# Turning the memory attention's weights by VectorE and DRAM instead of by TensorE

## The chip, the cores and the metric

The kernel runs on one core of a Trainium2 chip. Its engines are TensorE (PE; its weight loads are listed apart as PEld), VectorE (DVE), ScalarE (ACT), GpSimd (POOL) and SyncE (SP). They run independently, each through its own list of instructions in order, and wait for one another by semaphores. The metric is the device time of one execution in microseconds (us); less is better.

## What is computed

Two layers of a decoder trunk on 256 tokens of width 1024, all in 32-bit floats. Each layer is a SwiGLU half step, three token mixers in parallel, and another half step, with layer norms between. The three mixers (gated DeltaNet, sliding-window attention, attention to a memory of 256 rows) read one projection of the same stream, and their results are merged by gates:

```python
def memory_cross_attention(q, mem_n, w_mem_kv):
    ...
    s = jnp.einsum('bshd,bmhd->bhsm', q, k).astype(jnp.float32) * (XA_DH ** -0.5)
    p = jax.nn.softmax(s, axis=-1)
    o = jnp.einsum('bhsm,bmhd->bshd', p.astype(v.dtype), v)

def gated_delta_rule(q, k, v, g, beta):
    ...
    t_mat = a + jnp.eye(C, dtype=f32)
    sol = lax.linalg.triangular_solve(t_mat, rhs, left_side=True, lower=True, unit_diagonal=True)
    ...

merged = jnp.sum(gates * jnp.einsum('bsnc,ncd->bsnd', branches, w_branch), axis=2)
h = layer_norm(DEEPNORM_ALPHA * h + merged @ w_out, ln_g[1], ln_b[1])
```

Four heads of 128 attend to the memory. The change touches how `p` is turned for the second einsum, and the order of the work for the triangular solve.

## The kernel before

**Products.** Every product with a weight matrix is made of three matmuls: operands are split into a high part (rounded, `whi`, `hi`) and a low part (the rest, `wlo`, `lo`), and high x high, high x low and low x high are added up. Weights come from one long stream in DRAM in units of 128 x 1024 (`unit`). SyncE fetches a unit into one of four `raw` buffers, ScalarE rounds it (line 125), VectorE takes the difference (also line 125). There are five buffers for each half. The accumulators are four PSUM banks (`acc`); small products use `sm` and `at`, two banks each.

**Order.** In the mixers TensorE's instructions stand in program order (`keep_in_program_order`). The order is written out by `weave(work, steps)`: `work` is a run of large products in steps (one unit of weights each), and behind step n the functions in `steps[n]` are put, so that small work lies between large products. On the other engines a scheduler puts the instructions in order when the program is built, by its own estimate of the time; on the chip each engine then keeps that order. `tc.issue_after(i)` holds what is recorded under it behind the instruction `i`.

**Memory attention.** `x_scores(tb)` computes scores and softmax of token block tb (128 tokens) and leaves the weights in a tile `pp`, tokens on the partitions. `x_turn(tb)` turns them so that memory rows lie on the partitions: for each half `kb` of the memory four transposes of 128 x 128 on TensorE (line 137, into `at`), and one copy out of PSUM into a tile `pt` (line 749, by ScalarE for kb = 0, by VectorE for kb = 1). `x_values(tb)` multiplies with the memory's values and splits the result into high and low halves, `oX` (tiles `u6` and `u7`; line 125: ScalarE writes the high half, VectorE the low one).

**Delta inverses.** The triangular solve is done by building the inverse of each 128-block's matrix. `products` leaves the matrices in `AK` (tiles `u12`, `u13`). `inverses` starts with the 16 x 16 blocks on the diagonal: VectorE masks and sums them into `cp` (lines 826 and 827), GpSimd sends `cp` to DRAM (`dr`, line 829) and reads it back twice as a broadcast to all partitions (into `TM`, tiles `w2` and `w3`, line 833). GpSimd then eliminates in 15 steps of two operations (lines 845 and 846) and writes the first blocks of the inverse to `Y32` in tile `w0` (line 847). Eight mask products into `L32` (line 836) are GpSimd's too; the first matmuls of `doubling` read them. `begin_inverse` lets VectorE turn these blocks (line 940), behind the second `w_scores`. The doubling steps then run on TensorE.

**The place of the change.** `gates(0)` is eight steps of gate products; `branch(0, oX)` behind it projects the memory attention's result: four units of weights, then for block 0 and for block 1 two accumulators of 12 matmuls each, whose results VectorE takes out (line 1036). The matmuls of block 1 read the halves of `oX` that `x_values(1)` wrote. Transfers of GpSimd stand in its list like its other instructions: it waits there until their data are ready, issues them, and goes on. `leave_v` and `back_v` (lines 605 and 610) already turn other data the way that the change uses: VectorE's stream transpose turns each 32 x 32 block, four transfers bring the blocks to DRAM in the new order, and one reads them back.

Of the kernel before, what the change touches and what calls it, by code (L numbers as in the profile page):

```python
# [17 lines left out]
P = 128  # L18
# [20 lines left out]
def tile_trunk(ctx, tc, x, xT, mem, memT_, wst, lnp, memln, cvw, rows, cst, out):  # L39
# [484 lines left out]
    def mixers(l, hT, mkT, mv_, post):  # L524
# [197 lines left out]

        def x_scores(tb):
# [19 lines left out]
        def x_turn(tb):  # L743
            pT = prs[2 + tb] = T(p2, [P, 2, 4, P], "pt")
            for kb in range(2):
                ps = at().rearrange("p (h k) -> p h k", h=4)
                for h in range(4):
                    transpose(ps[:, h, :], prs[tb][:, h, kb * P:(kb + 1) * P], ident)
                (nc.vector.tensor_copy if kb else nc.scalar.copy)(pT[:, kb], ps)

        def x_values(tb):
            if not oX:
                oX.extend(T(pu, [P, 4, S], tag, F32R) for tag in ("u6", "u7"))
            ts = slice(tb * P, (tb + 1) * P)
            ps = at().rearrange("p (h k) -> p h k", h=4)
            for h in range(4):
                for kb in range(2):
                    matmul(ps[:, h, :], mv_[:, kb, h * P:(h + 1) * P], prs[2 + tb][:, kb, h, :], start=kb == 0, stop=kb == 1)
            split(oX[0][:, :, ts], oX[1][:, :, ts], ps)
# [61 lines left out]
        def inverses():  # L821

            cp = T(p2, [P, 2, 4, 16], "t2", bufs=4)
# [5 lines left out]
            nc.gpsimd.dma_start(dr, cp.rearrange("p c h i -> p (c h i)"))  # L829
            blocks = dr.rearrange("(d j) n -> d (j n)", j=16)  # L830
            for t in range(2):
                src = blocks[:, t * 1024:(t + 1) * 1024].unsqueeze(1).to_broadcast([8, 16, 1024])
                nc.gpsimd.dma_start(TM[t].rearrange("p a h c -> p (a h c)"), src)
            for c in range(2):
                for q in qd:
                    nc.gpsimd.tensor_tensor(L32[q, c], AK[c][q, :, 0, q], cs[q, C_LV:C_LV + 32].unsqueeze(1).to_broadcast([32, 4, 32]), op=ALU.mult)

            y16 = T(p2, [P, 8, 16], "t2", bufs=4)
            pr16 = T(p2, [P, 8, 15], "t2", bufs=4)
            i16 = cs[:, C_I16:C_I16 + 16].unsqueeze(1).to_broadcast([P, 8, 16])  # L840
            nc.gpsimd.tensor_copy(y16, i16)
# [22 lines left out]
        for kv in range(2):  # L864
# [5 lines left out]
            3: [lambda: spread(1)],  # L870
# [152 lines left out]
        def branch(n, o):  # L1023
# [19 lines left out]
            3: [lambda: x_turn(0)],  # L1043
            4: [lambda: x_values(0)],
            5: [lambda: x_turn(1)],
            6: [lambda: x_values(1)],
            7: [lambda: w_scores(0, 0)],
            8: [lambda: w_scores(0, 1)]})
# [193 lines left out]
```

## Time and profile before

| what | value |
|---|---|
| median of three runs | 1273.09 us (1271.39 to 1273.2) |
| the profiled execution's own time | 1271.84 us |
| its span, first to last instruction | 1270.1 us |
| granted TensorE clock, mean | 0.999 |
| TensorE busy | 1258.1 us |
| GpSimd busy | 221.0 us |

How to read the lines of the profile: the page gives, for each engine, busy time, share of the span and number of instructions; then the chain of work that ended last, followed back from the last instruction. A row of the timeline has start and length in us, engine, line, operation, result tile<-operand tiles, shapes and a count; in brackets stands the idle time of the engine just before it and what ended it. A row of a group ends with busy time and mean ns of one, then the idle time before. For transfers it gives the size of one and the median us from issue to landing. A row of the view by stretches has a stretch of time, the busy us of PE, PEld, DVE, ACT and POOL, the granted clock, and the share and speed of DMA.

### The profile page before, as it was taken

The page shows a single profiled execution, that of the slowest core. Times are in us where ns is not written, and L with a number is a line of the kernel's source. Part 1 is how long each engine was busy: PE and PEld are TensorE (multiplying, and loading weights), DVE is VectorE, ACT ScalarE, POOL GpSimd, SP SyncE. Part 2 cuts the span into 40 slices and gives each one's busy share as a digit, 9 for nine tenths or more (in the row PEclk, how much of TensorE's full clock was granted, in tenths as well). Part 3 has the DMA queues.
Part 4 walks back from the last instruction along what each step waited for, and adds up shares of the span by engine and source line. Part 5 has one row for each costly group of instructions (what it writes and reads, how often), then busy time and mean ns, then how long its engine had stood idle before and what let it go on. Part 6 is the DMA issues. An engine that isn't in the chain of part 4 may idle for free.

```text
span 1270.1 us, 18774 instructions
## 1 busy us (share of the span) xinstructions
PE 1258.1 (99%) x6916; PEld 1070.9 (84%) x6916; DVE 871.3 (69%) x1284; ACT 661.5 (52%) x982; POOL 221.0 (17%) x395
## 2 busy tenths in 40 slices
PE   9999999999999999999999999999999999999997
PEld 7888889999878888888888888899987788888886
DVE  6678576886667776665666665759776588766565
ACT  6456444655664544454454554455646654454441
POOL 1233000002331102221012220000023401122100
PEclk9999999999999999999999999999999999999999
DMA  8988765655554648787668887566554456578771
GB/s 293 322 265 286 249 210 160 205 179 137 164 151 150 240 139 258 243 242 220 215 208 246 256 255 216 178 185 212 162 158 133 134 189 226 174 248 243 240 231 74
DMA packets 78795, 263.56 MB, mean 208 GB/s; under 512 B 12528, under 2 KB 13968, under 8 KB 78704
## 3 DMA queue, kind: packets, MB, share of 16 engines
q1 hardware_dynamic: 66320, 232.40, 56.5%
q0 software_dynamic: 12240, 29.84, 8.7%
q8 instruction: 54, 0.88, 0.3%
q14 instruction: 37, 0.30, 0.1%
q10 hardware_dynamic: 144, 0.13, 0.0%
HBM read 247.48 MB, written 14.85 MB: 207 GB/s over the span
## 4 chain that ended last, share of the span: by engine, by line
PE 94%; DVE 3%; DMA 2%; ACT 1%; issue 1%; SPq 0%; DVEq 0%; ACTq 0%
PE acc L134 83%; PE at L134 3%; PE sm L134 3%; DMA raw<-in_wst_dram 2%; PE sm L137 1%; DVE wlo L125 1%; PE acc L335 1%; PE acc L332 1%; PE at L137 1%; PE acc L333 1%; ACT whi L125 1%; DVE h L291 0%; DVE h L296 0%; DVE h L418 0%; DVE bnst L277 0%
## 5 line engine op out<-in xcount | busy, mean ns | idle before, releaser
L125 DVE TENSOR_TENSOR wlo<-raw,whi 128x1024 fp32r<-128x1024 f32 (+2 forms) x405 | 487.1, 1210 | 277.0 <-ACT whi L125 275.0
L125 ACT CAST whi<-raw 128x1024 fp32r<-128x1024 f32 (+2 forms) x405 | 413.7, 1029 | 403.5 <-PE acc L134 314.8
L134 PE MATMUL acc<-whi,hT 128*128 128x512 f32 (+1 forms) x1824 | 563.1, 386 | 0.0
L134 PEld LDWEIGHTS acc<-whi,hT 128*128 128x128 f32 x1824 | 340.5, 188 | 68.9 <-issue 1.6
L134 PE MATMUL acc<-wlo,hT 128*128 128x512 f32 (+1 forms) x912 | 350.5, 384 | 0.1
L134 PE MATMUL acc<-whi,u 128*128 128x512 f32 x812 | 259.6, 392 | 0.0
L134 PEld LDWEIGHTS acc<-wlo,hT 128*128 128x128 f32 x912 | 171.6, 188 | 33.4 <-DVE wlo L125 0.9
L134 PEld LDWEIGHTS acc<-whi,u 128*128 128x128 f32 x812 | 152.3, 188 | 32.0 <-DVE u L125 0.5
L134 PE MATMUL acc<-wlo,u 128*128 128x512 f32 x406 | 158.2, 390 | 0.0
L362 POOL DMA_DIRECT2D tr<-t x176 | 96.0, 552 | 306.4 <-DVE t L356 299.4
L134 PE MATMUL acc<-hT,whi 128*128 128x256 f32 x672 | 121.8, 284 | 0.0
L134 PEld LDWEIGHTS acc<-hT,whi 128*128 128x128 f32 x672 | 104.7, 192 | 0.0
L134 PE MATMUL acc<-hT,wlo 128*128 128x256 f32 x336 | 95.1, 283 | 0.0
L134 PEld LDWEIGHTS acc<-wlo,u 128*128 128x128 f32 x406 | 76.3, 188 | 15.5
L134 PEld LDWEIGHTS acc<-hT,wlo 128*128 128x128 f32 x336 | 64.4, 192 | 0.0
L363 POOL DMA_DIRECT2D pt<-tr x44 | 25.0, 568 | 197.3 <-DMA tr<-t 151.6
L353 ACT ACTIVATE t<-acc 128x256 f32<-128x256 f32 x88 | 33.3, 379 | 37.1 <-PE acc L134 36.9
L134 PE MATMUL acc<-u,u 128*128 128x512 f32 x186 | 46.4, 394 | 0.0
L354 DVE TENSOR_TENSOR t<-t,acc 128x256 f32<-128x256 f32 x88 | 36.6, 417 | 8.1 <-ACT t L353 3.9
L134 PEld LDWEIGHTS acc<-u,u 128*128 128x128 f32 x186 | 34.6, 188 | 7.5
L553 DVE SCALAR_TENSOR_TENSOR t<-acc,cw,t 128x255 f32<-128x255 f32 (+2 forms) x72 | 34.5, 479 | 1.1
L125 DVE TENSOR_TENSOR u<-pt,u 128x512 fp32r<-128x512 f32 x44 | 28.9, 657 | 8.1 <-ACT u L125 8.1
(245 smaller groups left out, 1165.0 us busy)
## 6 DMA issues: line engine op xcount, KB each, us to landing
raw<-in_wst_dram SPq DMA_DIRECT2D x409, 512.0 KB, 4.4
tr<-t POOLq DMA_DIRECT2D x176, 64.0 KB, 3.9
pt<-tr POOLq DMA_DIRECT2D x44, 256.0 KB, 5.1
raw<-in_wst_dram SPq DMA_DIRECT2D x16, 324.0 KB, 3.0
gB<-in_lnp_dram SPq DMA_DIRECT2D x6, 512.0 KB, 6.7
bB<-in_lnp_dram SPq DMA_DIRECT2D x6, 512.0 KB, 7.0
w<-dr POOLq DMA_DIRECT2D x4, 512.0 KB, 12.6
t<-in_xT_dram SPq DMA_DIRECT2D x4, 256.0 KB, 5.4
```

What stands on the lines that cost most here:

```text
L125: return nc.scalar.copy(hi, src).ins, nc.vector.tensor_tensor(lo, src, hi.bitcast(F32), op=ALU.subtract).ins
L134: return pe(nc.tensor.matmul(*a, **k))
L137: return pe(nc.tensor.transpose(*a))
L332: nc.tensor.matmul(ps, hT[0][:, k, ts], hi[:, c], start=k == 0, stop=False)
L333: nc.tensor.matmul(ps, hT[0][:, k, ts], lo[:, c], start=False, stop=False)
L335: nc.tensor.matmul(ps, hT[1][:, k, ts], hi[:, c], start=False, stop=k == KD - 1)
L353: act = nc.scalar.activation(t[:, :, tb, :], g, AF.Silu).ins
L354: ins = nc.vector.tensor_tensor(t[:, :, tb, :], t[:, :, tb, :], u, op=ALU.mult).ins
L362: nc.gpsimd.dma_start(d[:, :, q].rearrange("b c x -> c b x"), z[32 * q:32 * q + 32].rearrange("c (b x) -> c b x", b=4))
L363: back = nc.gpsimd.dma_start(y, d.rearrange("b c q x -> (b c) (q x)")).ins
L553: nc.vector.scalar_tensor_tensor(yc[:, j, d:], b[:, j, :S - d], w[:, t:t + 1], yc[:, j, d:], op0=ALU.mult, op1=ALU.add)
```

## The change

The transposes of `x_turn` leave TensorE. VectorE turns the 32 x 32 blocks of each half of the weights, GpSimd sends them to DRAM by four transfers and reads them back by one (`square`). `x_turn(0)` now stands behind the third step of the run before `gates(0)`, ahead of `products(0, 0)`. `x_turn(1)` is no step of its own any more: `inverses` calls it and lays its transfers between its own, and `issue_after` ties GpSimd's list to that order, with the mask products behind all of them. `cp`, `y16` and `pr16` get tiles of their own. `x_values(0)` moves from step 4 to 5 of `gates(0)`, `w_scores(0, .)` from 7 and 8 to 6 and 7, and `x_values(1)` from 6 to 8, the last step ahead of `branch(0)`.

```diff
+        def square(src, dst, tag, after=None, bufs=2):
+
+            z = T(p2, [P, 512], "t2", bufs=4)
+            nc.vector.transpose(z, src)
+            d = T(pd, [4, 32, 4, P], tag, bufs=bufs)
+            for a in range(4):
+                nc.gpsimd.dma_start(d[:, :, a].rearrange("m x c -> x m c"), z[32 * a:32 * a + 32].rearrange("x (m c) -> x m c", m=4))
+            return lambda: nc.gpsimd.dma_start(dst, d.rearrange("m x a c -> (m x) (a c)"))
...
         def x_turn(tb):
-            pT = prs[2 + tb] = T(p2, [P, 2, 4, P], "pt")
-            for kb in range(2):
-                ps = at().rearrange("p (h k) -> p h k", h=4)
-                for h in range(4):
-                    transpose(ps[:, h, :], prs[tb][:, h, kb * P:(kb + 1) * P], ident)
-                (nc.vector.tensor_copy if kb else nc.scalar.copy)(pT[:, kb], ps)
+            pT = prs[2 + tb] = T(p2, [P, 2, 4, 4, 32], "pt")
+            backs = [lambda kb=kb: square(prs[tb][:, :, kb * P:(kb + 1) * P].rearrange("p h (m x) -> p m h x", m=4), pT[:, kb].rearrange("p a h x -> p (a h x)"), "tx", 4) for kb in range(2)]
+            if tb:
+                return backs
+            for f in [b() for b in backs]:
+                f()
...
-                    matmul(ps[:, h, :], mv_[:, kb, h * P:(h + 1) * P], prs[2 + tb][:, kb, h, :], start=kb == 0, stop=kb == 1)
+                    matmul(ps[:, h, :], mv_[:, kb, h * P:(h + 1) * P], prs[2 + tb][:, kb, :, h, :], start=kb == 0, stop=kb == 1)
...
-            nc.gpsimd.dma_start(dr, cp.rearrange("p c h i -> p (c h i)"))
+            sent = nc.gpsimd.dma_start(dr, cp.rearrange("p c h i -> p (c h i)")).ins
+
+            def then(f):
+                with tc.issue_after(sent):
+                    return f()
+
+            turns = x_turn(1)
+            backs = [then(turns[0])]
             blocks = dr.rearrange("(d j) n -> d (j n)", j=16)
             for t in range(2):
                 src = blocks[:, t * 1024:(t + 1) * 1024].unsqueeze(1).to_broadcast([8, 16, 1024])
-                nc.gpsimd.dma_start(TM[t].rearrange("p a h c -> p (a h c)"), src)
+                sent = then(lambda: nc.gpsimd.dma_start(TM[t].rearrange("p a h c -> p (a h c)"), src)).ins
+            backs.append(then(turns[1]))
+            for f in backs:
+                sent = then(f).ins
             for c in range(2):
                 for q in qd:
-                    nc.gpsimd.tensor_tensor(L32[q, c], AK[c][q, :, 0, q], cs[q, C_LV:C_LV + 32].unsqueeze(1).to_broadcast([32, 4, 32]), op=ALU.mult)
+                    ins = then(lambda: nc.gpsimd.tensor_tensor(L32[q, c], AK[c][q, :, 0, q], cs[q, C_LV:C_LV + 32].unsqueeze(1).to_broadcast([32, 4, 32]), op=ALU.mult)).ins
+            sent = ins
...
-            nc.gpsimd.tensor_copy(y16, i16)
+            with tc.issue_after(sent):
+                nc.gpsimd.tensor_copy(y16, i16)
...
-            3: [lambda: spread(1)],
+            3: [lambda: spread(1), lambda: x_turn(0)],
...
-            3: [lambda: x_turn(0)],
-            4: [lambda: x_values(0)],
-            5: [lambda: x_turn(1)],
-            6: [lambda: x_values(1)],
-            7: [lambda: w_scores(0, 0)],
-            8: [lambda: w_scores(0, 1)]})
+            5: [lambda: x_values(0)],
+            6: [lambda: w_scores(0, 0)],
+            7: [lambda: w_scores(0, 1)],
+            8: [lambda: x_values(1)]})
```

Numbers in the tile names below are those of buffers and instances. On GpSimd, from the mask products of layer 0 to the first operations of the elimination, the list was before:

```order
L836 TENSOR_TENSOR l32_465_2583<-u12_459_2575,cs_90 32x128 x4
L836 TENSOR_TENSOR l32_465_2583<-u13_460_2576,cs_90 32x128 x4
L841 COPY t2_529_3024<-cs_90 128x128
L829 DMA dr_528_3012<-t2_525_3005 128x128
L833 DMA w2_457_2573<-dr_528_3012 128x1x1024
L833 DMA w3_458_2574<-dr_528_3012 128x1x1024
L845 TENSOR_TENSOR t2_530_3025<-w2_457_2573,t2_529_3024 128x120
```

and is now, from the same transfer `dr` on (ahead of it stand the eight transfers out and two back of x_turn(0)):

```order
L838 DMA dr_533_3029<-cp_530_3022 128x128
L729 DMA tx_536_3034<-t2_535_3032 32x4x128 x4
L849 DMA w2_457_2573<-dr_533_3029 128x1x1024
L849 DMA w3_458_2574<-dr_533_3029 128x1x1024
L729 DMA tx_538_3043<-t2_537_3041 32x4x128 x4
L730 DMA pt_534_3031<-tx_536_3034 128x512
L730 DMA pt_534_3031<-tx_538_3043 128x512
L855 TENSOR_TENSOR l32_465_2583<-u12_459_2575,cs_90 32x128 x4
L855 TENSOR_TENSOR l32_465_2583<-u13_460_2576,cs_90 32x128 x4
L862 COPY y16_539_3058<-cs_90 128x128
L866 TENSOR_TENSOR pr16_540_3059<-w2_457_2573,y16_539_3058 128x120
```

The eight mask products stood ahead of `dr` and now stand behind the two reads back (`pt_534`), and so does the elimination; the second read back waits for the four transfers (`tx_538`) that are issued behind the broadcasts `w2` and `w3`.

On VectorE, around the stream transpose of `begin_inverse` (tile `w0`, which waits for the elimination's end), the list was before:

```order
L1036 SCALAR_TENSOR_TENSOR u4_586_3320<-gt_511_2939,acc_588_3322 128x512
L789 TENSOR_SCALAR mx_571_3278<-mx_571_3278 128x4
L1036 SCALAR_TENSOR_TENSOR u4_586_3320<-gt_511_2939,acc_589_3336 128x512
L792 TENSOR_TENSOR sums_572_3279<-sums_572_3279,sk_573_3280 128x4
L793 RECIPROCAL sums_572_3279<-sums_572_3279 128x4
L940 STREAM_TRANSPOSE w0_466_2584<-w0_466_2584 128x256
L125 TENSOR_TENSOR wlo_615_3488<-raw_613_3486,whi_614_3487 128x1024
```

and is now:

```order
L801 TENSOR_TENSOR sums_572_3256<-sums_572_3256,sk_573_3257 128x4
L802 RECIPROCAL sums_572_3256<-sums_572_3256 128x4
L961 STREAM_TRANSPOSE w0_466_2584<-w0_466_2584 128x256
L1057 SCALAR_TENSOR_TENSOR u4_590_3328<-gt_516_2956,acc_592_3330 128x512
L125 TENSOR_TENSOR u7_556_3171<-at_577_3293,u6_555_3170 128x4x128
L1057 SCALAR_TENSOR_TENSOR u4_590_3328<-gt_516_2956,acc_593_3344 128x512
L125 TENSOR_TENSOR wlo_619_3496<-raw_617_3494,whi_618_3495 128x1024
```

The two accumulators of block 0 in `branch(0)` (`u4`, line 1036, now 1057) and the low half of block 1's values (`u7_556` from `at_577`, the bank of `x_values(1)`) stood ahead of that transpose and now stand behind it. On TensorE, block 1 of `branch(0)` begins behind the first transposes of the sliding window's weights and reads that low half in its third matmul:

```order
L137 MATMUL at_595_3359<-cs_90,pp_561_3201 128x128 x4
L134 MATMUL acc_596_3365<-whi_579_3305,u6_555_3170 128x512
L134 MATMUL acc_596_3365<-wlo_580_3306,u6_555_3170 128x512
L134 MATMUL acc_596_3365<-whi_579_3305,u7_556_3171 128x512
L134 MATMUL acc_596_3365<-whi_582_3311,u6_555_3170 128x512
```

Here nothing moved: these five rows stand in the same order as before, with the waits on what ScalarE and VectorE wrote.

More of the change, by code (lines that the diff above doesn't have):

```diff
@@ L821, in inverses @@
         def inverses():
-            cp = T(p2, [P, 2, 4, 16], "t2", bufs=4)
+            cp = T(pu, [P, 2, 4, 16], "cp")
             for c in range(2):
@@ L832, in inverses @@
                 src = blocks[:, t * 1024:(t + 1) * 1024].unsqueeze(1).to_broadcast([8, 16, 1024])
-                nc.gpsimd.dma_start(TM[t].rearrange("p a h c -> p (a h c)"), src)
+                sent = then(lambda: nc.gpsimd.dma_start(TM[t].rearrange("p a h c -> p (a h c)"), src)).ins
+            backs.append(then(turns[1]))
+            for f in backs:
+                sent = then(f).ins
             for c in range(2):
                 for q in qd:
-                    nc.gpsimd.tensor_tensor(L32[q, c], AK[c][q, :, 0, q], cs[q, C_LV:C_LV + 32].unsqueeze(1).to_broadcast([32, 4, 32]), op=ALU.mult)
-            y16 = T(p2, [P, 8, 16], "t2", bufs=4)
-            pr16 = T(p2, [P, 8, 15], "t2", bufs=4)
+                    ins = then(lambda: nc.gpsimd.tensor_tensor(L32[q, c], AK[c][q, :, 0, q], cs[q, C_LV:C_LV + 32].unsqueeze(1).to_broadcast([32, 4, 32]), op=ALU.mult)).ins
+            sent = ins
+            y16 = T(pu, [P, 8, 16], "y16")
+            pr16 = T(pu, [P, 8, 15], "pr16")
             i16 = cs[:, C_I16:C_I16 + 16].unsqueeze(1).to_broadcast([P, 8, 16])
-            nc.gpsimd.tensor_copy(y16, i16)
+            with tc.issue_after(sent):
+                nc.gpsimd.tensor_copy(y16, i16)
             ab = [TM[c].rearrange("p a h (n i) -> p (a h) n i", i=16) for c in range(2)]
```

## The prediction

> **What bounds the kernel now.** I read the page from the top: the span, the busy shares, then the chain that ended last.
>
> ```profile
> span 1270.1 us, 18774 instructions
> PE 1258.1 (99%) x6916; PEld 1070.9 (84%) x6916; DVE 871.3 (69%) x1284; ACT 661.5 (52%) x982; POOL 221.0 (17%) x395
> PE 94%; DVE 3%; DMA 2%; ACT 1%; issue 1%; SPq 0%; DVEq 0%; ACTq 0%
> ```
>
> TensorE is busy nearly all the time and carries 94% of the chain, so an instruction taken from it is worth its own time, and a new wait of it costs its full length. GpSimd (POOL) is busy 17%: what it computes is cheap in sum, but it stands in one queue, in order, and the question is who waits for the end of that queue. Next come the chain in order of time (its pieces of the transposes that go) and, around them, the timelines of the engines in layer 0.
>
> ```profile
> 304.37 0.87 PE at L137 x8
> 312.52 0.87 PE at L137 x8
> ```
>
> These are the 16 transposes of the two x_turn calls of layer 0, on the chain.
>
> ```profile
> 294.94 2.51 POOL L836 TENSOR_TENSOR l<-u,cs 32x128 f32<-32x128 f32 x4 [14.35 <-DVE u L713]
> 301.51 3.42 POOL L836 TENSOR_TENSOR l<-u,cs 32x128 f32<-32x128 f32 x4 [4.06 <-DVE u L713]
> 305.00 0.29 POOL L841 COPY t<-cs 128x128 f32<-128x128 f32 x1
> 305.23 0.60 POOL L829 DMA_DIRECT2D dr<-t  x1
> 309.01 1.23 POOL L833 DMA_DIRECT2D w<-dr  x2 [3.18 <-DMA dr<-t]
> 319.59 0.40 POOL L845 TENSOR_TENSOR t<-w,t 128x120 f32<-128x120 f32 x1 [9.35 <-DMA w<-dr]
> 333.25 0.73 POOL L847 TENSOR_TENSOR w<-t,cs 128x256 f32<-128x256 f32 x1
> ```
>
> This is GpSimd's inverse: mask products, one transfer out (dr), two broadcasts back (w), then a chain of 31 operations from 319.59 to 333.98, 14.4 us. Its end is what VectorE waits for:
>
> ```profile
> 330.30 0.69 DVE L1036 SCALAR_TENSOR_TENSOR u<-gt,acc 128x512 f32<-128x512 f32 x1 [1.79 <-PE acc L134]
> 334.02 0.45 DVE L940 STREAM_TRANSPOSE w<-w 128x256 f32<-128x256 f32 x1 [2.75 <-POOL w L847]
> ```
>
> VectorE stood idle for 2.75 us at line 940 until GpSimd was done. It costs nothing now, because what TensorE needs next from VectorE stood ahead of it: both accumulators of token block 0 in branch(0) (line 1036; the second is the row above) and, long before, the low half of block 1's attention values. TensorE ran through:
>
> ```profile
> 330.99 0.63 PE L134 MATMUL acc<-whi,u 128*128 128x512 f32 x2
> 959.49 0.63 PE L134 MATMUL acc<-whi,u 128*128 128x512 f32 x2
> ```
>
> The first matmul of each row is the third of block 1 in branch(0), in layers 0 and 1: the first to read that low half. These two times are the marks that I measure against.
>
> **The change, part by part.** *Taken from TensorE:* 16 transposes a layer, 2 x 0.87 us, 3.5 us for both layers, if nothing else happened. With them go four copies on VectorE (0.69 each) and four on ScalarE; neither engine is the bound there.
>
> ```profile
> L749 DVE COPY pt<-at 128x512 f32<-128x512 f32 x4 | 2.8, 692 | 6.0 <-PE at L137 6.0
> L602 DVE STREAM_TRANSPOSE t<-u 128x512 f32<-128x512 f32 x4 | 2.5, 670 | 0.0
> ```
>
> *Added on VectorE:* eight stream transposes of 128x512, 0.67 us each by the second row. Of layer 0's four, two stand before the second block's products, so they push back the sum that dr carries. That sum ended at 303.2 (302.19 + 1.06); with the two transposes (1.3) and one weight split that now stands ahead of it (1.2) it ends at about 305.7.
>
> ```profile
> 292.01 0.90 ACT L739 ACTIVATE pp<-pp,sums 128x256 f32<-128x256 f32 x2
> 292.47 1.22 DVE L125 TENSOR_TENSOR wlo<-raw,whi 128x1024 fp32r<-128x1024 f32 x1
> 302.19 1.06 DVE L827 TENSOR_REDUCE t<-t 128x64 f32<-128x512 f32 x1
> 355.93 4.44 POOL L605 DMA_DIRECT2D tv<-t  x8
> 362.29 0.57 POOL L610 DMA_DIRECT2D u<-tv  x1 [1.91 <-DMA tv<-t]
> 364.04 0.56 POOL L610 DMA_DIRECT2D u<-tv  x1 [1.18 <-DMA tv<-t]
> ```
>
> *Added on GpSimd:* 16 transfers out and 4 back a layer. Their nearest rows are leave_v's and back_v's, of the same shapes: eight out in 4.44 us, the first read back 6.36 us after the first issue (362.29 - 355.93), the second 8.11 us after. For block 0 that is hidden: ScalarE ends the weights at 292.9, VectorE ends the split ahead at 293.7 and the first transpose by 294.4, so the reads back go at 300.7 and 302.5 and GpSimd is free at 303.1, before the sum at 305.7. So dr goes at 305.7, the four transfers of block 1's first half fit into its wait, and the broadcasts w go 3.78 us later as before, at 309.5, that is 0.5 late.
>
> *Moved behind w:* now the step that decides. After the two w stand, in this order on GpSimd: four transfers of block 1's second half, a read back, a second read back that **waits until those four have landed**, the eight mask products, a copy, and only then the 31 operations. How long do transfers take that are queued behind w?
>
> ```profile
> DMA to landing us min/median/max: 3.2/10.4/12.4
> DMA to landing us min/median/max: 3.3/12.7/13.2
> tr<-t POOLq DMA_DIRECT2D x176, 64.0 KB, 3.9
> u<-tv POOLq DMA_DIRECT2D x4, 256.0 KB, 3.2
> ```
>
> The first two rows are the three transfers dr, w, w of layers 0 and 1. The first w lands 10.4 us after its issue (at 319.4), the second, issued 0.6 us later, at 309.6 + 12.4 = 322.0: one after the other, not together. I take it that GpSimd's transfers go in turn, so the four behind them (256 KB, by the 2.6 us that 512 KB took in turn an estimated 1.3 us) land at 322.0 + 0.5 + 1.3 = 323.8. The bounds: 3.9 us after issue if they needn't queue (317.1 by leave_v's 6.36 from 310.7), 323.8 if they do; I take the upper end, because w itself behaves so. [...]
>
> The sum for layer 0: the second read back is issued at 323.8 and takes 0.6; mask products 2.51 + 3.42 = 5.9, which lay ahead of dr and were free and are now in line; the copy 0.3; the chain 14.4. Its end: 323.8 + 0.6 + 5.9 + 0.3 + 14.4 = **345.0 instead of 334.0**. Then, by the order of the new program, VectorE at its stream transpose holds back the first accumulator of branch(0) and the low half of block 1's values: 0.45 + 0.69 by the rows above, and 0.69 again for the low half, 1.8 us, so TensorE's mark comes at 346.8 instead of 331.0: **+15.8 us**. On the way TensorE waits for block 1's second read back too (issued by 324.4, landed 3.2 later at 327.6). It gets there at about 321: branch(0) began at 324.65, less the 1.7 saved and the 1.8 that the values take.
>
> ```profile
> 324.65 0.39 PE L134 MATMUL acc<-whi,u 128*128 128x512 f32 x1
> 316.15 1.78 PE at L134 x16
> ```
>
> That wait lies within the larger one, and so do the transposes' 1.7 us and whatever the values' matmuls lose by reading runs of 32: the mark is set by GpSimd. Only if GpSimd ended early would they count.
>
> ```profile
> 937.56 1.23 POOL L833 DMA_DIRECT2D w<-dr  x2 [3.27 <-DMA dr<-t]
> 950.40 0.40 POOL L845 TENSOR_TENSOR t<-w,t 128x120 f32<-128x120 f32 x1 [11.61 <-issue]
> 963.95 0.74 POOL L847 TENSOR_TENSOR w<-t,cs 128x256 f32<-128x256 f32 x1
> ```
>
> Layer 1: the second w lands at 938.2 + 13.2 = 951.4; + 0.5 + 1.3 + 0.6 + 5.9 + 0.3 + 14.3 (950.40 to 964.69) + 1.8 = 976.1 against 959.5: **+16.6 us**. Nothing behind the mark gives it back: the next units' splits wait for buffers that the same matmuls free, in both programs. SyncE's queue of weights has the same order as before.
>
> *The clock.* TensorE now stands still for about 10 us in one piece.
>
> ```profile
> 1264.00:1266.00 2.00, 0.00 (x0) 0.00 (x0) 1.90 (x6) 0.00 (x0) 0.00 (x0) 1.00 0.00 0
> 1266.00:1268.00 2.00, 0.00 (x0) 0.00 (x0) 0.62 (x2) 0.00 (x0) 0.00 (x0) 0.61 0.63 231
> 6.38 0.63 PE L134 MATMUL acc<-whi,hT 128*128 128x512 f32 x1
> 6.80 0.46 PE L134 MATMUL acc<-wlo,hT 128*128 128x512 f32 x1
> 330.77 0.39 PE L134 MATMUL acc<-wlo,u 128*128 128x512 f32 x1
> ```
>
> At the end of the kernel, where TensorE has no matmul after 1262, the granted clock falls below 1 in the stretch from 1266. At the start, matmuls of this shape start 0.42 us apart (6.38 to 6.80); at the mark they start 0.22 apart (330.77 to 330.99). So a stall of 10 us ends on a slow clock: between nothing and 5 us of half speed (from the first matmul at 1.5 to 6.8), a loss of 0 to 2.7; I take 2 a layer. [...]
>
> The sum, against the profiled execution's own 1271.84 us: + 15.8 + 16.6 + 4 = 1308.2. That execution lies 1.25 us under the median of the runs (1273.09), within their spread. I predict **1308 us**.
>
> **The rivals.** *Transfers behind w needn't queue.* Then the second read back goes at 317.1, masks end at 323.6, the copy at 323.9, the chain at 338.3, the mark at 340.1, +9.1 a layer; with the clock 1271.8 + 18.2 + 4 = 1294. For it: w's slowness may lie in w alone (it reads the same rows 16 times). Against it: the second w behind the first. Chance 0.20.
>
> *Only VectorE's order counts.* Transfers and masks all hide under w's landing: the chain starts at 320.1 and ends at 334.5, the mark is at 336.3, +5.3 a layer, 1271.8 + 10.6 + 2 = 1284. It needs masks done by 320, so block 1's transfers landed 0.8 us after their last issue at 312.9, against 3.9 in the rows. Chance 0.06.
>
> *Worse:* 512 KB more written and read in the same microseconds makes w itself slower; each microsecond costs 2 in all. At 3 us, 1314. Chance 0.09.
>
> *The other side: faster.* GpSimd's end is no bound, and TensorE keeps its 3.5 us: 1268.3. It decides at the point where GpSimd's chain ends 1.8 us before the mark, which itself comes 1.8 earlier: at 327.4, 6.6 us before today's end of 334.0, with a later w. The chain would have to take half its 14.4 us. Chance 0.05, a part of it within no change.
>
> **How the numbers follow.**
>
> ```profile
> L845 POOL TENSOR_TENSOR t<-w,t x15: 219/307/1223, 319.6 to 332.7; 128x120 f32<-128x120 f32 x1, 128x112 f32<-128x112 f32 x1, 128x104 f32<-128x104 f32 x1, 128x96 f32<-128x96 f32 x1
> L846 POOL TENSOR_TENSOR t<-t,t x15: 217/317/1389, 320.1 to 333.0; 128x120 f32<-128x120 f32 x1, 128x112 f32<-128x112 f32 x1, 128x104 f32<-128x104 f32 x1, 128x96 f32<-128x96 f32 x1
> ```
>
> The forecast, 1302 to 1315 with its bounds (clock 0 to 2.7 a layer, the transfers' 1.3 us, a chain 2 us shorter while VectorE stands still, since two of its operations took 1.2 and 1.4 us where the median is 0.3), has 0.60. To hold 8 in 10 the range reaches to the first rival with some room: **1290 to 1315**. A measurement of this kernel can tell about 0.2% from no change: faster by more 0.03, within 0.02, slower by more 0.95.
>
> **What would show it.** VectorE's stream transpose (line 961 of the changed kernel) idle for some 15 to 20 us for GpSimd; GpSimd's first chain operation at about 330.6 instead of 319.6, with a wait before the last read back of some 10 us for the transfers ahead; TensorE's third matmul of block 1 waiting for VectorE at about 346; the clock under 1 behind it; no L137 rows that write at from the x_turn line. Wrong would be: the wait before the last read back under 5 us (first rival), or no wait of TensorE between 321 and 347 at all (then GpSimd's chain was shorter than its rows say).

## The result, and the profile after

| | before | after |
|---|---|---|
| median of five runs | 1272.02 us (1270.21 to 1273.2) | 1302.02 us (1301.06 to 1305.39) |
| ratio, 95% interval | | 1.0239 (1.0226 to 1.0252) |
| the profiled execution, and its span | 1271.84, 1270.1 us | 1301.06, 1299.2 us |
| granted TensorE clock, mean | 0.999 | 0.987 |

The change costs 30 us. From the page of the changed kernel: busy time of the engines, and the chain that ended last by engine.

```profile
PE 1264.5 (97%) x6884; PEld 1074.1 (83%) x6884; DVE 871.4 (67%) x1288; ACT 658.8 (51%) x978; POOL 235.5 (18%) x435
PE 86%; DMA 4%; DVE 3%; POOL 3%; issue 2%; ACT 1%; SPq 0%; DVEq 0%; POOLq 0%; ACTq 0%
```

TensorE executes 32 matmuls fewer and is yet busy 6.4 us longer (the granted clock is 0.987 on the mean, where it was 0.999); GpSimd, not on the chain before, has 3% of it, and DMA 4% instead of 2%. (Line numbers are those of the changed kernel: 849 issues w, 729 and 730 the new transfers out and back, 855 the masks, 866 to 868 the elimination, 961 is VectorE's turn of w0.) Where this happens is in GpSimd's timeline of layer 0 (start, length, engine, line; idle time before and what ended it in brackets):

```profile
309.17 1.24 POOL L849 DMA_DIRECT2D w<-dr  x2 [1.30 <-DMA dr<-cp]
310.40 2.24 POOL L729 DMA_DIRECT2D tx<-t  x4
325.68 0.57 POOL L730 DMA_DIRECT2D pt<-tx  x1 [12.48 <-DMA tx<-t]
326.26 4.11 POOL L855 TENSOR_TENSOR l<-u,cs 32x128 f32<-32x128 f32 x8
330.80 0.40 POOL L866 TENSOR_TENSOR pr<-w,y 128x120 f32<-128x120 f32 x1
342.51 0.73 POOL L868 TENSOR_TENSOR w<-y,cs 128x256 f32<-128x256 f32 x1
```

The last read back waits 12.48 us for four transfers issued behind w; masks and a copy follow, and the elimination runs from 330.80 to 343.24, where it ran from 319.59 to 333.98. VectorE and TensorE behind it, in their own timelines:

```profile
343.28 0.45 DVE L961 STREAM_TRANSPOSE w<-w 128x256 f32<-128x256 f32 x1 [18.22 <-POOL w L868]
```

```profile
326.62 0.77 PE L134 MATMUL at<-pt,u 128*128 128x128 f32 x2 [5.91 <-DMA pt<-tx]
328.67 3.36 PE L134 MATMUL at<-pt,u 128*128 128x128 f32 x14 [1.28 <-DMA pt<-tx]
344.95 1.22 PE L134 MATMUL acc<-whi,u 128*128 128x512 f32 x2 [5.95 <-DVE u L125]
357.52 1.08 PE L134 MATMUL at<-pt,swv 128*64 128x512 f32 x4 [0.20 <-DVE pp L788]
987.04 1.22 PE L134 MATMUL acc<-whi,u 128*128 128x512 f32 x2 [5.73 <-DVE u L125]
999.42 1.08 PE L134 MATMUL at<-pt,swv 128*64 128x512 f32 x4 [0.20 <-DVE pp L788]
```

TensorE waits twice a layer: for block 1's read backs ahead of x_values(1), and at the mark (the third row, at 344.95) for the low half that VectorE computes behind its turn of w0. The row at 357.52 is the first of the sliding window's values, w_values(0); the kernel before has it at 340.98 and, in layer 1, at 970.34:

```profile
340.98 1.08 PE L134 MATMUL at<-pt,swv 128*64 128x512 f32 x4 [0.18 <-DVE pp L779]
970.34 1.08 PE L134 MATMUL at<-pt,swv 128*64 128x512 f32 x4 [1.04 <-DVE pp L779]
```

So layer 0 loses 16.5 us up to there and layer 1 another 12.5 (29.1 less 16.5), together the whole growth of the span, 29.1 us. In sum nothing is lost or won elsewhere.

### The profile page after: what moved, and what is told of

The parts are those of the page before. It is cut to its first block, busy times and chain, and to the rows that moved or that the text cites. A ratio compares the mean times of both kernels' runs of the same rounds, so it can differ in the third digit from the quotient of the medians.

```text
span 1299.2 us, 18789 instructions
## 1 busy us (share of the span) xinstructions
PE 1264.5 (97%) x6884; PEld 1074.1 (83%) x6884; DVE 871.4 (67%) x1288; ACT 658.8 (51%) x978; POOL 235.5 (18%) x435
## 4 chain that ended last, share of the span: by engine, by line
PE 86%; DMA 4%; DVE 3%; POOL 3%; issue 2%; ACT 1%; SPq 0%; DVEq 0%; POOLq 0%; ACTq 0%
PE acc L134 78%; PE sm L134 2%; PE at L134 2%; DMA tx<-t 2%; DMA raw<-in_wst_dram 2%; DVE wlo L125 1%; PE sm L137 1%; PE acc L335 1%; POOL y L867 1%; PE acc L332 1%; POOL pr L866 1%; PE acc L333 1%; ACT whi L125 1%; DMA dr<-cp 1%; POOL l L855 1%
## 5 line engine op out<-in xcount | busy, mean ns | idle before, releaser
L134 PE MATMUL acc<-whi,u 128*128 128x512 f32 x812 | 263.9, 398 | 11.7 <-DVE u L125 11.7
L125 ACT CAST u<-pt 128x512 fp32r<-128x512 f32 x44 | 27.0, 613 | 16.4 <-DMA pt<-tr 16.4
```

What stands on the lines that cost most here:

```text
L125: return nc.scalar.copy(hi, src).ins, nc.vector.tensor_tensor(lo, src, hi.bitcast(F32), op=ALU.subtract).ins
L134: return pe(nc.tensor.matmul(*a, **k))
```

## Experiments

All ratios are to the kernel before; the changed kernel stands at 1.0239.

| run | what differs | median, us | ratio (95%) |
|---|---|---|---|
| e6 | before, with VectorE's order of the change | 1284.61 | 1.0116 (1.0099 to 1.0132) |
| e3 | changed, VectorE's order as before | 1288.84 | 1.0142 (1.0128 to 1.0155) |
| e1 | changed, masks early | 1290.85 | 1.0149 (1.0134 to 1.0164) |
| e2 | changed, transfers out ahead of w | 1285.17 | 1.0109 (1.0096 to 1.0122) |
| e4 | e2 and e3 together | 1283.68 | 1.0097 (1.0079 to 1.0115) |
| e7 | e4, read backs ahead of w too | 1286.23 | 1.0127 (1.0112 to 1.0142) |
| e5 | changed, four transfers on ScalarE's queue | 1291.2 | 1.0164 (1.0143 to 1.0184) |
| e8 | e4, w on ScalarE's queue | 1284.59 | 1.0107 (1.0090 to 1.0124) |
| e9 | e4, second w behind the read backs | 1280.08 | 1.0072 (1.0059 to 1.0085) |
| e10 | e9, masks early | 1279.62 | 1.0069 (1.0050 to 1.0088) |
| e11 | e10, x_values(1) one accumulator later | 1274.35 | 1.0022 (1.0011 to 1.0032) |

### VectorE's order: e6 and e3

e6 takes the kernel before and gives VectorE the order of the change (with TensorE's, x_values(1) behind w_scores, from which it follows); e3 takes the changed kernel and holds the turn of w0 behind the low half and block 0's accumulators again. The edit of e6, on the kernel before:

```diff
-            split(oX[0][:, :, ts], oX[1][:, :, ts], ps)
+            with (tc.issue_after(wpr["inv"]) if tb else nullcontext()):
+                split(oX[0][:, :, ts], oX[1][:, :, ts], ps)
...
-                nc.vector.transpose(W[:, 512:768], W[:, 768:1024])
+                wpr["inv"] = nc.vector.transpose(W[:, 512:768], W[:, 768:1024]).ins
...
-            6: [lambda: x_values(1)],
-            7: [lambda: w_scores(0, 0)],
-            8: [lambda: w_scores(0, 1)]})
+            6: [lambda: w_scores(0, 0)],
+            7: [lambda: w_scores(0, 1)],
+            8: [begin_inverse, lambda: x_values(1)]})
...
-            3: [lambda: w_turn(0, 1), begin_inverse],
+            3: [lambda: w_turn(0, 1)],
```

And e3, on the changed kernel (`wpr["low", 1]` is the instruction that writes block 1's low half, `wpr["b0"]` the last one that VectorE has taken out of an accumulator by then, and `issue_after` holds the turn behind both):

```diff
-            split(oX[0][:, :, ts], oX[1][:, :, ts], ps)
+            wpr["low", tb] = split(oX[0][:, :, ts], oX[1][:, :, ts], ps)[1]
...
-            with tc.issue_after(wpr["end"]):
+            with tc.issue_after(wpr["end"]), tc.issue_after(wpr["low", 1]), tc.issue_after(wpr["b0"]):
...
-            2: [lambda: w_turn(0, 0)],
+            2: [lambda: w_turn(0, 0), lambda: wpr.update(b0=late["dve"])],
```

> The kernel before, TensorE's transposes kept and GpSimd untouched, with one order on VectorE alone: w_scores ahead of x_values(1), and the turn of w0 ahead of x_values(1)'s low half and block 0's accumulators, as the changed kernel has them. GpSimd's elimination ends at about 334 as before. Theory: VectorE stands at the turn until 334, the low half and the accumulator follow, the mark comes at 336 to 337 instead of 331.0: 4 to 6 us a layer with the clock, 1279 to 1284 us. Rival, that order costs nothing by itself (a wait taken up elsewhere): 1271 to 1273. Rival, it costs as much as the whole change, the late transfers being beside the point: 1297 to 1303.

> The changed kernel, with one order on VectorE moved back: the turn of w0 (the first instruction of the delta inverse there) is held behind the low half of x_values(1) and block 0's accumulators, where the kernel before has it. GpSimd's order and its transfers stay as in the changed kernel, so the elimination ends as late, at about 343. Queue theory with VectorE's order as what passes the delay on: the mark no longer waits; TensorE waits for the read backs ahead of x_values(1), some 6 to 7 us with half a clock behind, and the first doubling, some 16 us later, finds the turn done or nearly: 1287 to 1292 us. Rival, the late elimination is itself on the path whatever VectorE's order (the doublings or the inverses' products wait for it): 1298 to 1302.

TensorE in e6 (the marks of both layers), then TensorE and, by itself, VectorE in e3:

```profile
336.80 1.22 PE L134 MATMUL acc<-whi,u 128*128 128x512 f32 x2 [5.02 <-DVE u L125]
974.03 1.22 PE L134 MATMUL acc<-whi,u 128*128 128x512 f32 x2 [6.40 <-DVE u L125]
```

```profile
326.96 0.77 PE L134 MATMUL at<-pt,u 128*128 128x128 f32 x2 [5.92 <-DMA pt<-tx]
349.56 0.65 PE L134 MATMUL at<-pt,swv 128*64 128x512 f32 x2 [1.00 <-DVE pp L788]
```

```profile
343.94 0.45 DVE L961 STREAM_TRANSPOSE w<-w 128x256 f32<-128x256 f32 x1 [5.19 <-POOL w L868]
```

In e6 GpSimd does nothing new, no transfer is added, the mark comes where it was expected (336.8), and the kernel still loses 1.2%: the order alone (VectorE's, with TensorE's that goes with it) puts a wait of 5.0 and 6.4 us on TensorE. That is half a microsecond over the expectation. e3 is where it was expected: the elimination is as late as in the changed kernel (VectorE's turn at 343.94), yet the wait at the mark is gone and only 1.00 us appears at the row of w_values(0); what is left is the wait for the read backs. By ratios, order alone costs 1.2% and the rest alone 1.4%, against 2.4% together: nearly a sum.

### GpSimd's line: e1 and e2

In e1 the mask products are no longer held behind the last read back:

```diff
-                    ins = then(lambda: nc.gpsimd.tensor_tensor(L32[q, c], AK[c][q, :, 0, q], cs[q, C_LV:C_LV + 32].unsqueeze(1).to_broadcast([32, 4, 32]), op=ALU.mult)).ins
-            sent = ins
+                    nc.gpsimd.tensor_tensor(L32[q, c], AK[c][q, :, 0, q], cs[q, C_LV:C_LV + 32].unsqueeze(1).to_broadcast([32, 4, 32]), op=ALU.mult)
```

In e2 block 1's transfers all go out ahead of w (`last["out"]` is the last of them, kept in `square`), both read backs stay behind w:

```diff
-            backs = [then(turns[0])]
+            backs = [then(t) for t in turns]
+            sent = last["out"]
...
-            backs.append(then(turns[1]))
```

> The changed kernel, with one thing undone: the eight mask products are no longer held behind the last read back on GpSimd, so that they run early, as in the kernel before. Queue theory (GpSimd's instructions stand in line behind its last read back of block 1, which waits for transfers behind the two w; VectorE's turn of w0 waits for the elimination, and block 1's low half and accumulators behind that turn): the elimination starts right behind the wait at about 326.3 us instead of 330.8, the mark (TensorE's third matmul of block 1 in the first delta branch) comes at about 340.5 instead of 345.0, and the same in layer 1: 4.1 to 4.6 us a layer less, 1293 to 1295 us. Rival, VectorE's order alone or the clock alone costs the time: no change, 1301 to 1303. Rival, w itself sets the start: w has landed before 326, so it would give the same 1293 to 1295 and is not told apart here.

> The changed kernel, with the four outgoing transfers of block 1's second square issued ahead of the two w on GpSimd's queue instead of behind them; the order on VectorE as in the changed kernel. Queue theory: the last read back finds its data landed at about 314 to 316 us (325.7 in the changed kernel), the masks run while w travels, the elimination starts when w lands, 321 to 323, and ends at 333.5 to 335.5; the mark at 336 to 338, so 5 to 7 us a layer over the kernel before and 8 to 9 under the changed kernel: 1282 to 1287 us. Rival, the transfers are slow wherever they stand (a turn by DRAM of this pattern takes 12 us, or w takes from them whatever the order): the last read back still waits to 323 or later, 1297 to 1302. Rival, w becomes late by as much as the others become early: the elimination starts at 327 to 329, 1291 to 1296.

GpSimd and TensorE in e1:

```profile
326.72 0.40 POOL L865 TENSOR_TENSOR pr<-w,y 128x120 f32<-128x120 f32 x1
```

```profile
340.85 0.73 PE L134 MATMUL acc<-whi,u 128*128 128x512 f32 x2 [0.76 <-DVE u L125]
350.99 1.08 PE L134 MATMUL at<-pt,swv 128*64 128x512 f32 x4 [0.19 <-DVE pp L788]
```

The elimination starts 4.1 us earlier and so does the mark, as expected; the time, 1290.85 us, is below the expected 1293 to 1295, because a wait of 0.76 us in place of 5.95 leaves the clock alone (granted 1.00 from 336 to 352, where the changed kernel has 0.50 from 344 to 348 and 0.72 to 352): from mark to the later row take 10.1 us, in the changed kernel 12.6. GpSimd in e2:

```profile
315.89 0.57 POOL L730 DMA_DIRECT2D pt<-tx  x1 [1.52 <-DMA tx<-t]
323.40 1.11 POOL L866 TENSOR_TENSOR pr<-w,y 128x120 f32<-128x120 f32 x1 [0.55 <-DMA w<-dr]
```

Ahead of w the same four transfers land in time for a read back at 315.89 instead of 325.68, and the median is inside the expected range. The rival that they are slow wherever they stand falls. But the time comes about in another way than expected, so that the fit is in part luck. TensorE in e2:

```profile
326.28 0.59 PE L134 MATMUL at<-pt,u 128*128 128x128 f32 x2 [4.41 <-DVE sums L802]
338.38 0.63 PE L134 MATMUL acc<-whi,u 128*128 128x512 f32 x2
```

Both read backs now stand behind w and land 12.4 and 11.8 us after their issue. TensorE stands 4.41 us ahead of x_values(1): the first read back lands at about 326.2 (the row names VectorE, whose sums end at the same time; in layer 1, where TensorE waits 4.14 us, the row names the read back). At the mark, 338.38, it does not wait any more.

### Both together, and why that was not enough: e4, e7

> Both edits together: the outgoing transfers of block 1 ahead of the two w on GpSimd's queue, and the turn of w0 behind the low half of x_values(1) and block 0's accumulators on VectorE. Queue theory: block 1 is back before TensorE comes to x_values(1), the elimination ends at about 334 to 335 us, before a doubling needs it, and nothing is left of the delay; TensorE is without its 32 transposes, some 3.5 us: 1268 to 1271 us, 0.1 to 0.3% faster than the kernel before. Rival, turning by way of DRAM is late in itself (the last read back, or block 0's, comes after TensorE whatever the order): 1276 to 1290. Rival, TensorE's saving is hidden because another engine sets the end of these stages: 1271 to 1273, no change.

This missed: 1283.7 us, 13 over what the theory gave and inside the rival's range (runs from 1278.79, the profiled one, to 1287.04). GpSimd and TensorE in e4:

```profile
313.91 0.59 POOL L730 DMA_DIRECT2D pt<-tx  x1 [0.33 <-DMA tx<-t]
315.92 0.57 POOL L730 DMA_DIRECT2D pt<-tx  x1 [1.43 <-DMA tx<-t]
```

```profile
324.48 0.46 PE L134 MATMUL at<-pt,u 128*128 128x128 f32 x2 [2.42 <-DMA pt<-tx]
325.66 3.27 PE L134 MATMUL at<-pt,u 128*128 128x128 f32 x14 [0.72 <-DMA pt<-tx]
```

GpSimd waits little (0.33 and 1.43 us), but now, as in e2, the read backs are what stands behind w: issued at 313.91 and 315.92, they let TensorE go at 324.5 and 325.7, 10 us later. e7 moves w behind them:

```diff
-            sent = last["out"]
+            for f in backs:
+                sent = then(f).ins
...
             for t in range(2):
...
                 sent = then(lambda: nc.gpsimd.dma_start(TM[t].rearrange("p a h c -> p (a h c)"), src)).ins
-            for f in backs:
-                sent = then(f).ins
```

> Out first and turn late together, with the two w moved once more: behind both read backs of block 1 on GpSimd's queue, so that nothing of block 1 stands behind w. Queue theory: the read backs land 4 to 6 us after their issue, 318 to 321, and TensorE does not wait at x_values(1) (2.4 and 0.7 us with w ahead of them); w, issued at about 316.5, lands at 327 to 329, the elimination ends at 340 to 342, and the turn of w0, behind the low half and the accumulators, is late by at most 1 us for the products of the delta inverse: 1268 to 1271 us. Rival, the read backs are slow in themselves (10 us of 512-byte pieces, whatever stands ahead): TensorE still waits 2 to 3 us, 1275 to 1284. Rival, the elimination's later end is itself on the path: 1274 to 1282 with no wait of TensorE at x_values(1), and a wait for VectorE behind.

The issues of e7 from 303 to 330 (size, median us from issue to landing), then VectorE and TensorE:

```profile
w<-dr POOLq DMA_DIRECT2D x2, 512.0 KB, 11.0
pt<-tx POOLq DMA_DIRECT2D x3, 256.0 KB, 3.2
```

```profile
340.52 0.45 DVE L960 STREAM_TRANSPOSE w<-w 128x256 f32<-128x256 f32 x1 [11.28 <-POOL w L867]
```

```profile
346.13 1.97 PE L134 MATMUL at<-pt,swv 128*64 128x512 f32 x4 [7.09 <-DVE pp L788]
```

Ahead of w the read backs land 3.2 us after their issue by the median (block 1's two, issued at 313.10 and 316.41, and one of block 0) and TensorE does not wait at x_values(1), at 321.07 and in layer 1 at 957.87 (0.43 us there at x_values(0)). But w, issued at 317, ends the elimination at 340.5, and TensorE, which is now early, waits 7.09 us behind VectorE's turn, at a granted clock of 0.50 from 344 to 352 behind it. This is the third case of the expectation, larger than it was put (1274 to 1282): I had read e3's slack at the turn as the program's, but TensorE was late there itself.

### A queue or the DMA engines: e5, e8

In e5, on the changed kernel, `square` gets the engine that issues its transfers out (ScalarE for block 1's second half):

```diff
-                nc.gpsimd.dma_start(d[:, :, a].rearrange("m x c -> x m c"), z[32 * a:32 * a + 32].rearrange("x (m c) -> x m c", m=4))
+                (out or nc.gpsimd).dma_start(d[:, :, a].rearrange("m x c -> x m c"), z[32 * a:32 * a + 32].rearrange("x (m c) -> x m c", m=4))
...
```

In e8, on e4, w goes to ScalarE:

```diff
-                sent = then(lambda: nc.gpsimd.dma_start(TM[t].rearrange("p a h c -> p (a h c)"), src)).ins
+                then(lambda: nc.scalar.dma_start(TM[t].rearrange("p a h c -> p (a h c)"), src))
```

> The changed kernel, with the four outgoing transfers of block 1's second square issued on ScalarE's queue, in time still behind the two w, which stay on GpSimd's queue ahead of both read backs. Queue theory (what is behind w on the same queue waits for w, what is on another does not): the four transfers land within about 5 us of their issue, so the last read back no longer waits to 325.7 but is issued at 314 to 318, the masks lie beside w, and the elimination starts at 321 to 324; the read backs themselves, still behind w on GpSimd's queue, land only 8 to 11 us after their issue. 1282 to 1289 us. Rival, the transfers wait for w because both share the DMA engines or the rows in DRAM, not the queue: they land 10 us or more after their issue on ScalarE's queue too, the last read back waits to 322 or later, 1293 to 1302.

> Out first and turn late together, with the two w on ScalarE's queue, issued there at about 310 to 312, ahead of the read backs in time but not in their queue. Queue theory: the read backs land 4 to 6 us after their issue, 318 to 321, TensorE does not wait at x_values(1), the elimination starts when the masks are through or w has landed, 322 to 324, and ends at about 335: 1268 to 1271 us. Rival, w holds up the read backs by the DMA engines and not by the queue: they land at 323 to 326 as with w ahead of them on GpSimd's queue, TensorE waits 2 to 3 us a layer, 1276 to 1284. Rival, ScalarE's wait for w's data holds its casts: 1272 to 1276 with TensorE waiting for ScalarE at 310 to 315.

ScalarE's queue and GpSimd in e5; the same in e8, with TensorE:

```profile
307.45 1.32 ACTq L729 DMA_DIRECT2D tx<-t  x3
309.62 0.31 ACTq L729 DMA_DIRECT2D tx<-t  x1
319.05 0.57 POOL L730 DMA_DIRECT2D pt<-tx  x1 [4.89 <-DMA tx<-t]
```

```profile
309.17 1.79 ACTq L850 DMA_DIRECT2D w<-dr  x2
313.37 0.57 POOL L730 DMA_DIRECT2D pt<-tx  x1 [2.52 <-DMA tx<-t]
318.15 0.56 POOL L730 DMA_DIRECT2D pt<-tx  x1 [4.21 <-DMA tx<-t]
323.04 0.46 PE L134 MATMUL at<-pt,u 128*128 128x128 f32 x2 [1.52 <-DMA pt<-tx]
326.71 3.36 PE L134 MATMUL at<-pt,u 128*128 128x128 f32 x14 [3.21 <-DMA pt<-tx]
```

In e5 three of the four transfers left ahead of w (issued at 309.26 on GpSimd's queue), so the run shows less than was meant; the fourth, behind the first w on another queue, held the last read back to 319.05, 9.4 us after its issue; the time lies between the two expectations. In e8 the read backs stand alone on GpSimd's queue and TensorE still gets their data 9.7 and 8.6 us after their issue, against 10.6 and 9.7 in e4. Giving w a queue of its own saves a microsecond or so and not the 5 that the queue theory asked for: it falls. In layer 1 w, issued at 943.6 beside block 1's transfers out, delays these too (they land 8.5 us after their issue by the median, 4.6 in e4), so that the read backs go at 953.11 and 956.85 (947.50 and 949.50 in e4) and TensorE waits 7.31 us; the time is no better than e4's. The last rival falls as well: in layer 0 TensorE waits nowhere for ScalarE between 300 and 320. The profile counts all queues in the time of the same 16 DMA engines: from 311 to 322 (queues told apart by their sizes) SyncE's takes 45.9% of it, ScalarE's 26.3 and GpSimd's 23.5, together 96%, and from 316 to 320 it is full (view by stretches, e8; the last three columns are clock, share, which as the profile counts it can pass 1, and GB/s):

```profile
316.00:320.00 4.00, 4.00 (x23) 3.42 (x21) 3.49 (x8) 1.88 (x7) 1.68 (x4) 1.00 1.04 235
```

While w travels the read backs come nearly as late on another queue than w's (8.6 to 9.7 us after their issue, e8) as on the same (9.7 to 10.6, e4). The transfers share the DRAM that they read as well; no run tells whether they wait for that or for the DMA engines.

### How far it can be mended: e9, e10, e11

e9 keeps only the first w ahead of the read backs (on e4):

```diff
             for t in range(2):
+                for f in backs if t else []:
+                    sent = then(f).ins
...
-            for f in backs:
-                sent = then(f).ins
```

e10 adds e1's edit; e11 also moves x_values(1) behind block 0's first accumulator:

```diff
-            8: [lambda: x_values(1)]})
...
+            1: [lambda: x_values(1)],
             2: [lambda: w_turn(0, 0), lambda: wpr.update(b0=late["dve"])],
```

> Out first and turn late together, with only the second of the two w (which the elimination reads from its ninth step on) moved behind both read backs of block 1 on GpSimd's queue; the first w stays ahead of them. Theory (w is slow by what it asks of the DMA engines, whichever queue issues it, and what follows it in time lands after it): one w takes about half of the 10 us that two take, so the read backs land about 5 to 7 us after their issue, at 319 to 322, and TensorE, which comes to x_values(1) at 322, waits at most 0.5 us; the first w has landed before the masks end (322.5), the second before it is read at about 330, so the elimination ends at 334.5 to 336 as with both w ahead: 1268 to 1273 us, and the profile within 2 us of the kernel before. Rival, the read backs wait for the DMA engines even behind one w (landing at 323 or later): 1276 to 1284. Rival, the second w comes too late for the ninth step: GpSimd stands in the middle of the elimination, which ends at 338 or later, and TensorE waits for VectorE's products behind it: 1276 to 1286.

> The same, with the mask products early as in the kernel before (between block 0's two read backs), so that nothing stands between the last read back and the elimination but the first w. Theory: dr goes out about 0.5 us later, the elimination starts when the first w has landed, 318.5 to 321, instead of behind the masks at 322.6, and ends at 331 to 334 unless the second w holds it: 1267 to 1270 us, up to 0.3% faster than the kernel before. Rival, the masks were not what the elimination waited for (w lands at 322 or later): the same time as with the masks late. Rival, block 0's second read back, behind the masks, is late for x_values(0): a wait of TensorE of 1 us or more at about 310, 1272 to 1276.

> The version before (first w ahead of the read backs, second behind, masks early, turn of w0 late), with TensorE's order changed at one place: x_values(1) stands behind block 0's first accumulator of the first delta branch instead of ahead of it, some 2.7 us later; the accumulators need its result only from block 1 on. Theory (all that is left of the change's cost is TensorE's wait for the read backs, 2.1 and 1.5 us in layer 0, 0.7 and 2.1 in layer 1, and the clock behind it): TensorE comes at about 324.0 instead of 321.3, the read backs land at 323.3 and 325.3, so at most 1.5 us of wait a layer is left, and the 32 transposes' 3.5 us come through: 1268 to 1274 us. Rival, the elimination, which ends at about 335, is late for a TensorE that no longer waits, so that VectorE's turn holds its weights' low halves: the wait moves to the products behind the turn, 1274 to 1280.

GpSimd and TensorE in e10; TensorE in e11 (layer 0, then layer 1):

```profile
311.10 0.64 POOL L852 DMA_DIRECT2D w<-dr  x1
322.04 0.40 POOL L865 TENSOR_TENSOR pr<-w,y 128x120 f32<-128x120 f32 x1 [4.89 <-DMA w<-dr]
```

```profile
323.31 0.46 PE L134 MATMUL at<-pt,u 128*128 128x128 f32 x2 [2.06 <-DMA pt<-tx]
```

```profile
324.45 1.98 PE L134 MATMUL at<-pt,u 128*128 128x128 f32 x16
340.85 1.08 PE L134 MATMUL at<-pt,swv 128*64 128x512 f32 x4 [1.11 <-DVE pp L788]
955.34 2.17 PE L134 MATMUL at<-pt,u 128*128 128x128 f32 x14 [2.60 <-DMA pt<-tx]
```

e9's and e10's theory missed: the first w takes as long as two did (issued at 311.10, needed and waited for until 322.04), so the read backs behind it are hardly earlier, and the masks' place no longer matters (1.0072 and 1.0069, intervals that overlap). e11's missed narrowly: with TensorE coming 2.7 us later the wait in layer 0 is gone, the one in layer 1 is not, and 1274.35 us lies 0.35 above what was expected, in the rival's range, 0.2% above the kernel before. A part of the rival's wait is there too: VectorE makes its turn at 335.23, and TensorE waits 1.11 us for what VectorE does behind it (row at 340.85). No version beat the kernel before; the transposes' 3.5 us are still eaten by 2.6 us of waiting in layer 1, 1.1 in layer 0 and the clock (granted 0.91 from 950 to 970, 1.00 in the kernel before).

## Why the prediction was right, point by point

1308 us was predicted, 1290 to 1315 as the range; 1302.02 was measured. Mechanism, place and sign held; the sum was 6 to 7 us too large.

- **The last read back waits behind w.** Predicted issue 323.8, measured 325.68 (+1.9). In layer 1 it went at 967.74, which is 951.2 without the 16.5 us of layer 0, 2.0 before the predicted 953.2:

```profile
967.74 0.56 POOL L730 DMA_DIRECT2D pt<-tx  x1 [8.59 <-DMA tx<-t]
```

The landing times of dr and the two w in layers 0 and 1 show why; before they were 10.4 and 12.4, then 12.7 and 13.2:

```profile
DMA to landing us min/median/max: 3.5/13.0/14.3
DMA to landing us min/median/max: 3.8/9.1/9.9
```

Behind the second w's landing the read back goes 1.6 and 2.1 us later, where 0.5 + 1.3 was predicted. That this came so near is partly luck: the 1.3 was half of the 2.6 us that lay between the landings of the two w in layer 0, read as one after the other, but in layer 1 the same rows give 1.1, and in the changed kernel it is 1.9 and 1.4.

- **Its reason was too narrow.** The prediction had "GpSimd's transfers go in turn", an estimate from the landings of the two w in the kernel before (10.4 and 12.4 us). The bound held, but e8 shows that another queue is no way round: the DMA engines' time is full while w travels (share 0.87 from 312 to 316, 1.04 from 316 to 320), and what is issued behind it comes late on either queue (8.6 to 9.7 us, and 9.7 to 10.6). Nor is the first of the two w much faster when the second is held back: e10's first w, with the read backs behind it and the second issued 5 us after it, takes 10.9 us, so that to keep only one ahead (e9) gained little. What one w takes with nothing beside it, no run shows.
- **Masks 5.9, chain 14.4.** Mis-sized: 4.11 and 12.44 (330.80 to 343.24) in layer 0, about the same in layer 1. These two terms, 3.8 us in layer 0 and 3.6 in layer 1, are the whole error of 7; the two misses of the read back, +1.9 and -2.0, cancel, which is luck. The prediction had named the chain's 2 us as a bound, not the masks'.
- **VectorE 1.8:** 1.7 (343.24 to 344.95). e6 and e3 show that its order carries the elimination's delay to TensorE.
- **The mark:** +14.0 for +15.8 in layer 0, +11.0 for +16.6 in layer 1 (987.04 - 959.49 - 16.5).
- **The clock, 2 a layer**, a choice between the bounds 0 and 2.7: from mark to the row at 357.52 take 12.6 us where 10.0 were, and in layer 1 12.4 where 10.9 were: 2.6 and 1.5. The 10.9 hold a wait of 1.04 us at the later row (970.34) that is 0.20 in the changed kernel, so the slow clock itself took about 2.4 in layer 1. The stretches of the changed kernel show it, after both waits:

```profile
328.00:332.00 4.00, 3.33 (x15) 3.33 (x16) 0.00 (x0) 0.00 (x0) 3.40 (x9) 0.50 0.01 3
344.00:348.00 4.00, 3.05 (x7) 2.50 (x8) 1.49 (x3) 0.00 (x0) 0.00 (x0) 0.50 0.00 0
```

- **The first wait lies within the larger one:** so it was (5.91 and 1.28 us, then still 5.95 at the mark). TensorE came at 320.7 (326.62 - 5.91); 321 was predicted. But e2, e3 and e4 show that this wait counts in full once the larger one goes.
- **Rivals.** "Transfers needn't queue" asked for a wait under 5 us before the last read back; it is 12.48. "Only VectorE's order" is a part, not the whole (e6). "Worse" asked for a w some 3 us slower: the second took 1.9 us longer in layer 0, but 3.3 less in layer 1. "Faster" would need the read backs by 321 and the elimination's end at about the old time at once; e7 reaches the first, e2 and e4 nearly the second (it starts at 323.4 in e2), and each loses at the other.

## What to carry to other kernels

Here 3.5 us taken from the busiest engine ended as a loss of 29, with what replaces them put behind a transfer (w) that lands 9 to 14 us after its issue: ask which transfers are under way ahead of the new ones, not only which queue they stand in (e8: read backs 8.6 to 9.7 us on another queue, 9.7 to 10.6 on the same in e4). Work that "hides" in an idle engine's list delays all that follows it in that list (e1: without the mask products ahead of it the elimination starts 4.1 us earlier); compare the new end of the list with what the bound engine reads next, and with what stands behind the waiting instruction on the engine between. An order that leaves a long wait in front of something urgent can cost about as much as the late data itself (e6: 1.2% with no new transfer; e3: 1.4% with the transfers and without that order).

## What the hardware showed beside that

**GpSimd's mask products went faster where VectorE stood still.** In the changed kernel, where VectorE is all but idle beside them (in layer 0 busy for 0.34 us from 324 to 328 and not at all to 332), one takes 440 to 466 ns, the median 445. In e2, where VectorE is busy for 3.65 of the 4 us from 320 to 324 (least, median and largest ns of one):

```profile
L855 POOL TENSOR_TENSOR l<-u,cs x16: 446/458/1417, 316.5 to 957.4; 32x128 f32<-32x128 f32 x16
```

The median is nearly the same, but beside a busy VectorE single ones take 1.4 us; eight take 4.1 us in the one and 6.0 in the other. Whether VectorE's work is the cause is not shown: no run here separates it from others.

**w is slow without the change, too.** In the kernel before, where none of the new transfers exist, it takes 10.4 to 13.2 us. In e7, where it goes last, it still takes 11 us. DMA queues of e7 from 320 to 328 (packets, MB, share of the 16 engines' time):

```profile
q0 software_dynamic: 543, 1.05, 78.2%
q1 hardware_dynamic: 104, 0.36, 24.0%
```

A megabyte of the first (mostly w) takes 0.782 x 8 x 16 / 1.05 = 95 us of one DMA engine. One of the second (weights) takes 0.24 x 8 x 16 / 0.36 = 85 in the same stretch, but 52 from 340 to 348, without w (53.8% for 1.33 MB). So while w travels the weights' transfers take longer too, and it is not shown whether w's packets are slow in themselves or only because so many are under way. Whether that comes from reading the same rows 16 times was not tried.
